# Values of three attention heads projected 512 columns at a time in a one-core hybrid attention and recurrence layer

## The chip, the cores and the metric

The kernel runs on one core of one Trainium2 chip. A core has a matrix engine (TensorE, written PE in the profile, its weight loads PEld), a vector engine (VectorE, DVE), a scalar engine (ScalarE, ACT), GpSimd (POOL) and SyncE (SP), which here only issues DMAs. Each engine works through its own queue in order and waits on semaphores for the others. The metric is the device time of one execution, in microseconds (us).

## The reference, cut to what matters

One layer over 512 latent tokens and 256 context tokens, 2048 features, all in float32. Every token is normalised and modulated, and one input projection makes queries, keys, values, gates and the input of a recurrent branch. What concerns us is the value part `v`, 2048 columns, for four heads of 512 columns each, and for both streams:

```
hn = rmsnorm(h, g_norm) * (1.0 + scale) + shift
parts = split(hn @ w_in, bounds)              # parts[2] is v: GLA_HEADS * GLA_DV = 4 * 512 columns
v = split_heads(parts[2], GLA_DV)
o_gla, ... = gla_bidir(q, k, v, la_f, la_b, s0_f, s0_b)      # attention of each head
y_rnn, ... = rglru_bidir(xc, ...)                             # recurrent branch, 16 blocks of 128 features
out = rmsnorm(x + gt * merge_out(...), g_final)
```

The attention reads `v` of the context and of the latents; the recurrent branch reads neither. So the values can be made anywhere before the head that needs them.

## The kernel before, in words

Every product is made of three matmuls: operands are split into a leading and a remaining part (`hi`, `lo`, type fp32r), and `mm3` (L130) adds hi times hi, hi times lo and lo times hi. ACT makes `whi` from a raw weight piece and DVE makes `wlo` (`hilo`, L121). A piece is [128, 1024] floats, loaded by one DMA; three split pieces are in a ring, and each piece is split two pieces ahead of its matmuls (`run`, L209).

The program has four phases. Phase 0 makes the modulation, the normalised tokens (`xhi`, `xlo` for the latents, `chi`, `clo` for the context) and the keys. Phase 1 makes all that reads the context too: for each of eight `j` a group `g_feat` of the recurrent input (R, both streams), one of its gate (GR, latents only), and after these the groups of values that the table `VALUES_AT` names. Phase 2 makes queries (Q), output gates (G) and merge gates (M) of the latents, 28 groups of 96 matmuls each. Phase 3 is the output projections.

In a group of values before the change (`g_tok`, L273), 256 columns are made at once: the tokens' tile of 128 is the stationary operand, the weights are the moving one, 256 wide. There are eight groups of four pieces; one piece takes 6 token tiles x 4 feature tiles x 3 = 72 matmuls. The sums of four latent tiles lie in two PSUM banks of the pool `px` (four banks), those of the two context tiles in one bank of `pc` (two banks). `evac_v` (L851) then copies bank by bank to `vt` on ACT, two buffers, and POOL sends each `vt` to memory (`vS`), from where the attention reads it back.

Beside the main stream runs side work, written as generators: in phase 1 one `rnn_block` (L898) for each of 16 blocks of the recurrent branch, appended when its GR group ends, and a `gate_row` (L994) at two places; in phase 2 the attention of the four heads (`gla_all`), one after the other. A step of it is put into the program at a `yield` of the main stream, when a rough clock of the engines (`T`, with `rdy`, `lim` and `slack`, in `run_side`, L163) finds that what the step needs will be there. `g_tok` yields after every 6 matmuls of 256 columns. Whatever is left is put in at once, ready or not, by `flush_side` (L199): at the first piece of phase 2 (`to_gla`) and when the first piece of phase 3's input is loaded (`swap`), because the memory pools of the finished phase are closed there. In between, `need` forces side steps where a buffer must be free.

Names in the rows: `rx` and `rc` are the block products of `rnn_block` (latents and context; four pairs in a block, each pair in the same two banks `sa` and `sb`), `g` what ACT makes of them, `xc`, `xh`, `xl`, `wr`, `wh`, `wl` their operands; `pr` and `grow` belong to `gate_row`, whose one `grow` buffer is sent to memory twice, and `pr` uses bank `sa` too; `po` are the output sums of a head, `dg` with `oss` their squares, `on` the normalised sums, `pt` their transposes, `sgg` the gated result.

Of the kernel before, what the change touches and what calls it, by code (L numbers as in the profile page):

```python
# [5 lines left out]
F32 = mybir.dt.float32  # L6
# [6 lines left out]
P = 128  # L13
# [8 lines left out]
# columns of the packed per-feature parameters  # L22
# [5 lines left out]
# weight pieces: [128, 1024] each  # L28
# [13 lines left out]
# the modulation's blocks of feature tiles, and the runs (group, feature tiles) of the keys' products that follow  # L42
# [3 lines left out]
# which groups of the values follow a group of the recurrent branch  # L46
VALUES_AT = [(), (0,), (1,), (2,), (3,), (4,), (), (5, 6, 7)]
# [8 lines left out]
class Kern:  # L56
    def __init__(self, tc, a, out):
        self.tc, self.nc, self.a, self.out = tc, tc.nc, a, out
        self.side = []
        self.pend = ()  # L60
        # a rough clock of the engines as the program is written down: when each is done with what it was given,
        # and when each tile is ready
        self.T = {"pe": 0.0, "dve": 0.0, "act": 0.0}
        self.rdy = {}
        self.table = None
        self.lim, self.slack = 4.0, 1.0
        self.conv_done = self.gr_done = self.q_done = self.heads_done = 0

# [55 lines left out]
    def mm(self, out, lhsT, rhs, start, stop, share=1):  # L124
        # share: how many column tiles of the array work at once
        n = self._n(rhs)
        self._op("pe", (n / 2400.0 + 0.003 if n >= 256 else 0.213) / share, out, lhsT, rhs)
        self.nc.tensor.matmul(out, lhsT=lhsT, rhs=rhs, start=start, stop=stop, skip_group_check=True)  # L128
# [7 lines left out]
    def rstd(self, out, ss, n, tmp):  # L136
        # 1/sqrt(ss/n + eps), the estimate polished by one Newton step
        v, y = tmp[:, 0], tmp[:, 1]
        self.ts(v, ss, 1.0 / n, EPS, ALU.mult, ALU.add)
        self.act(y, v, AF.Sqrt)  # L140
        self.nc.vector.reciprocal(out=y, in_=y)
        self.tt(out, y, y, ALU.mult)
        self.tt(out, out, v, ALU.mult)
        self.ts(out, out, -0.5, 1.5, ALU.mult, ALU.add)
        self.tt(out, out, y, ALU.mult)

# [37 lines left out]
    @staticmethod  # L184
    def zipg(*gens):
        """emit independent chains in turns."""
        gens = list(gens)
        while gens:
            for g in list(gens):
                try:  # L190
                    yield next(g)
                except StopIteration:
                    gens.remove(g)
# [10 lines left out]
    def prime(self, pieces):  # L204
        """the first pieces of the stream to come."""
        self.primed = len(pieces)
        for p in pieces:
            self.load(p)
        return lambda: [self.do_split(p) for p in pieces]  # L209
# [28 lines left out]
    def g_feat(self, w0, evac, ctx, pre=None):  # L238
        """two feature tiles of 128 columns, features on partitions."""
# [33 lines left out]
    def g_tok(self, w0, evac):  # L273
        """256 columns, tokens on partitions, both streams."""
        st = {}
        ps = []

        def mk(pi):
            def mm(hi, lo):
                if pi == 0:  # L280
                    st["x"] = [self.px.tile([P, 2, 256], F32, tag="px", name="px") for _ in range(2)]
                    st["c"] = self.pc.tile([P, 2, 256], F32, tag="pc", name="pc")
                h = hi.rearrange("p (k c) -> p k c", c=256)
                l = lo.rearrange("p (k c) -> p k c", c=256)
                for seg in range(3):
                    for kk in range(4):
                        if kk or seg:
                            yield
                        k = pi * 4 + kk
                        for j in range(2):  # L290
                            if seg < 2:
                                o, t0, xh, xl = st["x"][seg], (2 * seg + j) * P, self.xhi, self.xlo
                            else:
                                o, t0, xh, xl = st["c"], j * P, self.chi, self.clo
                            self.mm3(o[:, j, :], (xh[:, k, t0:t0 + P], xl[:, k, t0:t0 + P]),
                                     (h[:, kk, :], l[:, kk, :]), k == 0 and j == 0, k == KT - 1)
            return mm

        for pi in range(4):
            ps.append(Piece(self.a["w"][w0 + pi], mk(pi), (lambda: evac(st["c"], *st["x"])) if pi == 3 else None))  # L300
        return ps

# [1 line left out]
    def build(self):  # L304
# [44 lines left out]
        # phase 0: modulation, normalised tokens, keys  # L349
# [17 lines left out]
        # phase 1: everything that reads the context as well  # L367
        pcs[0].before = to_rnn
        main = []
        for j in range(8):  # L370
            main += self.g_feat(W_R + 4 * j, self.evac_r(j), True)
            main += self.g_feat(W_GR + 4 * j, self.evac_gr(j), False)
            for i in VALUES_AT[j]:
                main += self.g_tok(W_V + 4 * i, self.evac_v(i))
# [8 lines left out]
        # phase 2: projections of the latents only, attention beside them  # L383
# [22 lines left out]
        # phase 3: output projections  # L406
# [52 lines left out]
    def start(self, sp, raw0, raw, prime):  # L459
        """modulation, normalised tokens in feature-major form, and the keys, whose products follow the tokens  # L460
        feature tile by feature tile: the features come in chunks, and between chunks partial sums wait in SBUF."""
# [18 lines left out]
        # columns c, cctx, and zeros  # L480
# [11 lines left out]
        # the tokens, features on partitions: two feature tiles of the latents or four of the context in each  # L492
# [6 lines left out]
        todo = []          # [earliest start, task] of other engines than the tensor engine  # L499
        hot = []           # the same of the tensor engine, to be done at once  # L500
        rk = {}            # when feature tile (k, stream) is split
# [37 lines left out]
        def rstd(s, r):  # L539
            # the sum of squares of each token on its own partition, and 1/sqrt(mean + eps)  # L540
# [16 lines left out]
        def spread(s, g, r):  # L557
            # the factors of all tokens along the free axis, on every partition
# [50 lines left out]
        def ada():  # L609
# [8 lines left out]
            for kk in range(kn):  # L618
                # four parts of the sum in the array's four column tiles
# [56 lines left out]
        for c, (g, ks) in enumerate(runs):  # L676
            its = [(k, s, c2) for k in ks for s in range(2) for c2 in range(2)]
            if c == 0:
                # the latents of two tiles before the context
                its[2:6] = its[4:6] + its[2:4]  # L680
# [17 lines left out]
        def ksplit_soon():  # L698
            # a piece can be split when its load is there and a place in the ring is free
# [20 lines left out]
        def where(g):  # L720
            """where the sums of a group wait: four banks of the latents, two of the context, in place of what
            has become of the tokens."""
# [96 lines left out]
    def la_pieces(self):  # L819
        st = {}  # L820
        ps = []
        for pi in range(2):
            def conv(raw, pi=pi):
                # columns of each 128: the weights' leading parts three times, their remainders once
# [17 lines left out]
            def post():  # L842
                # rows 0-63 the leading products rounded (twice), 64-95 what the rounding left, 96-127 the others
# [7 lines left out]
    def evac_v(self, j):  # L851
        def f(c, x0, x1):
            h, o = j // 2, (j % 2) * 256
            for i, t in enumerate((c, x0, x1)):
                s = self.rp.tile([P, 2, 256], F32, tag="stg", name="vt", bufs=2)
                self.act(s, t)
                self.nc.gpsimd.dma_start(out=self.vS[h, :, 2 * i:2 * i + 2, o:o + 256], in_=s)
        return f
# [22 lines left out]
    def decay_consts(self):  # L881
        """-8 * softplus(-lam), log1p by the odd series of atanh."""
# [165 lines left out]
    def gla_z(self, h):  # L1048
        """pre-activations of the log decays of head h."""
# [17 lines left out]
    def gla_log(self, h):  # L1067
        """log decays times 16, summed along each block of 128 tokens."""
# [35 lines left out]
    def gla_scores(self, h):  # L1104
# [16 lines left out]
        def make_ctx(d):  # L1121
            """queries and keys whose products reach over to the context, queries' own blocks."""
# [6 lines left out]
            # decays over whole blocks between the pair: context to latents, latents' blocks, context's blocks  # L1129
# [82 lines left out]
        def make_qd(d):  # L1212
            """diagonal blocks, decays against the middle of the block."""
# [44 lines left out]
        def mm_diag(d):  # L1258
# [13 lines left out]
            # key index on partitions, query index on the free axis  # L1272
# [153 lines left out]
    def g_final(self, j):  # L1426
# [13 lines left out]
        def loads(pi):  # L1440
            # a part beside each of the first pieces
# [28 lines left out]
        for pi in range(8):  # L1470
# [26 lines left out]
            def post():  # L1497
# [3 lines left out]
                if j == 2:  # L1501
                    # sums of squares so far, with eps
# [7 lines left out]
    def finish(self, t):  # L1510
# [12 lines left out]
        if t < 3:  # L1523
            # the vector engine has the next tile's sums to take up
# [16 lines left out]
def pack(i):  # L1541
    """Lay the inputs out for the chip: pieces in the order in which they are read."""
# [5 lines left out]
    def g256(w):  # [2048, n*256] -> [n*4, 128, 1024]  # L1548
# [3 lines left out]
    def g512(w):  # [2048, n*512] -> [n*8, 128, 1024]  # L1552
# [3 lines left out]
    c = lambda a, b: w_in[:, a:b]  # L1556
    w = np.concatenate([
        g512(c(1024, 2048)), g256(c(2048, 4096)), g256(c(6176, 8224)), g256(c(8224, 10272)),
# [55 lines left out]
```

## Time and profile before

| what | value |
|---|---|
| median of 3 runs | 2339.16 us (2339.06 to 2339.24) |
| span of the profiled execution | 2337.9 us from first to last instruction |
| PE busy | 2291.6 us, 98% |
| DVE busy | 1153.3 us, 49% |
| ACT busy | 1004.6 us, 43% |

The profile gives the span of one execution. The runs' median lies 1.3 us above it, which is what lies around the first and the last instruction and is taken to stay. A matmul's duration in the trace is longer than the distance to the next one, since matmuls overlap: what a matmul costs is read from the starts of a run of them. An engine's idle time is listed with what ended it.

### The profile page before, as it was taken

The page shows a single profiled execution, that of the slowest core. Times are in us where ns is not written, and L with a number is a line of the kernel's source. Part 1 is how long each engine was busy: PE and PEld are TensorE (multiplying, and loading weights), DVE is VectorE, ACT ScalarE, POOL GpSimd, SP SyncE. Part 2 cuts the span into 40 slices and gives each one's busy share as a digit, 9 for nine tenths or more (in the row PEclk, how much of TensorE's full clock was granted, in tenths as well). Part 3 has the DMA queues.
Part 4 walks back from the last instruction along what each step waited for, and adds up shares of the span by engine and source line. Part 5 has one row for each costly group of instructions (what it writes and reads, how often), then busy time and mean ns, then how long its engine had stood idle before and what let it go on. Part 6 is the DMA issues. An engine that isn't in the chain of part 4 may idle for free. (4 is left out here: it accounts for less than half of the span.)

```text
span 2337.9 us, 29156 instructions
## 1 busy us (share of the span) xinstructions
PE 2291.6 (98%) x12008; PEld 1919.1 (82%) x12008; DVE 1153.3 (49%) x1464; ACT 1004.6 (43%) x1309; POOL 137.3 (6%) x217
## 2 busy tenths in 40 slices
PE   4999999999999999999999999999999999999998
PEld 2557889899988988998888888888888888888786
DVE  5223345566555665555645637637633423434334
ACT  4222244554545545556545646564534311222223
POOL 1222000000000000000000000000000000000000
PEclk8999999999999999999999999999999999999999
DMA  7663323333333333223233233223335533333523
GB/s 299 239 221 118 108 70 107 122 104 119 114 116 104 113 126 109 77 95 128 93 131 108 77 122 117 93 97 118 105 114 200 196 118 118 117 126 136 191 92 117
DMA packets 84406, 296.72 MB, mean 127 GB/s; under 512 B 10160, under 2 KB 11312, under 8 KB 83376
## 3 DMA queue, kind: packets, MB, share of 16 engines
q1 hardware_dynamic: 72656, 256.04, 31.9%
q0 software_dynamic: 11616, 38.81, 4.7%
q8 instruction: 94, 1.54, 0.3%
q14 instruction: 40, 0.33, 0.0%
HBM read 264.40 MB, written 30.42 MB: 126 GB/s over the span
## 5 line engine op out<-in xcount | busy, mean ns | idle before, releaser
L95 DVE TENSOR_TENSOR wlo<-raw,whi 128x1024 fp32r<-128x1024 f32 x304 | 374.8, 1234 | 569.7 <-ACT whi L91 568.2
L91 ACT ACTIVATE whi<-raw 128x1024 fp32r<-128x1024 f32 x304 | 320.8, 1057 | 538.0 <-PE px L128 329.5
L128 PE MATMUL px<-xhi,whi 128*128 128x512 f32 x1408 | 551.5, 392 | 0.0
L128 PE MATMUL px<-xhi,wlo 128*128 128x512 f32 x1408 | 549.0, 390 | 0.0
L128 PE MATMUL px<-xlo,whi 128*128 128x512 f32 x1408 | 548.1, 389 | 0.0
L128 PEld LDWEIGHTS px<-xhi,wlo 128*128 128x128 f32 x1408 | 264.2, 188 | 57.3
L128 PEld LDWEIGHTS px<-xhi,whi 128*128 128x128 f32 x1408 | 264.4, 188 | 54.0 <-issue 2.6
L128 PEld LDWEIGHTS px<-xlo,whi 128*128 128x128 f32 x1408 | 264.4, 188 | 51.6
L128 PE MATMUL px<-whi,xhi 128*128 128x256 f32 x512 | 144.8, 283 | 0.0
L128 PE MATMUL px<-wlo,xhi 128*128 128x256 f32 x512 | 144.8, 283 | 0.0
L128 PE MATMUL px<-whi,xlo 128*128 128x256 f32 x512 | 144.7, 283 | 0.0
L91 ACT ACT_TABLE_LOAD x101 | 129.6, 1283 | 1.8
L128 PE MATMUL px<-wlo,mhi 128*128 128x512 f32 x256 | 101.1, 395 | 0.8 <-DVE wlo L95 0.8
L128 PE MATMUL px<-whi,mhi 128*128 128x512 f32 x256 | 101.1, 395 | 0.0
L128 PE MATMUL px<-whi,mlo 128*128 128x512 f32 x256 | 101.0, 394 | 0.0
L128 PE MATMUL px<-yhi,whi 128*128 128x512 f32 x256 | 100.9, 394 | 0.0
L128 PE MATMUL px<-yhi,wlo 128*128 128x512 f32 x256 | 100.4, 392 | 0.0
L128 PE MATMUL px<-ohi,whi 128*128 128x512 f32 x256 | 99.6, 389 | 0.0
L128 PE MATMUL px<-ohi,wlo 128*128 128x512 f32 x256 | 99.6, 389 | 0.0
L128 PE MATMUL px<-olo,whi 128*128 128x512 f32 x256 | 99.6, 389 | 0.0
L128 PE MATMUL px<-ylo,whi 128*128 128x512 f32 x256 | 99.3, 388 | 0.0
L128 PEld LDWEIGHTS px<-wlo,xhi 128*128 128x128 f32 x512 | 98.1, 192 | 0.2
(320 smaller groups left out, 3959.4 us busy)
## 6 DMA issues: line engine op xcount, KB each, us to landing
raw<-in_w SPq DMA_DIRECT2D x304, 512.0 KB, 3.6
araw<-in_wss SPq DMA_DIRECT2D x64, 512.0 KB, 4.9
raw<-in_wgt SPq DMA_DIRECT2D x32, 512.0 KB, 4.2
gS<-mst POOLq DMA_DIRECT2D x32, 256.0 KB, 2.5
gst<-gS POOLq DMA_DIRECT2D x32, 256.0 KB, 3.0
kraw<-in_w POOLq DMA_DIRECT2D x14, 512.0 KB, 5.5
vS<-vt POOLq DMA_DIRECT2D x24, 256.0 KB, 2.8
st<-vS SPq DMA_DIRECT2D x12, 512.0 KB, 4.7
```

The source lines that it names most:

```text
L91: return self.nc.scalar.activation(out=out, in_=in_, func=func, **kw)
L95: return self.nc.vector.tensor_tensor(out=out, in0=in0, in1=in1, op=op)
L128: self.nc.tensor.matmul(out, lhsT=lhsT, rhs=rhs, start=start, stop=stop, skip_group_check=True)
```

## The change

Heads 0, 1 and 3 are projected by a new group `g_head`: 512 columns at once, eight pieces of two feature tiles each, and a PSUM bank for each of the six token tiles (all four of `px` and both of `pc`). Every tile is copied out as soon as its last matmul is issued. Head 2 stays with `g_tok`, in two groups. The table now puts heads 0 and 1 after j = 1 and 3, the halves of head 2 after j = 5 and 7, and head 3 last. `g_head` yields after every 6 matmuls of 512 columns: five times in a piece, where `g_tok` yields eleven times. The weights are laid out on the host to match.

```
-VALUES_AT = [(), (0,), (1,), (2,), (3,), (4,), (), (5, 6, 7)]
+VALUES_AT = [(), (("w", 0),), (), (("w", 1),), (), (("n", 4),), (), (("n", 5), ("w", 3))]
...
+    def g_head(self, w0, evac):
+        st = {}
+        ps = []
+        def mk(pi):
+            def mm(hi, lo):
+                if pi == 0:
+                    st["o"] = [self.px.tile([P, 512], F32, tag="px", name="px") for _ in range(4)] + \
+                              [self.pc.tile([P, 512], F32, tag="pc", name="pc") for _ in range(2)]
+                for t in range(6):
+                    if t:
+                        yield
+                    xh, xl = (self.xhi, self.xlo) if t < 4 else (self.chi, self.clo)
+                    t0 = (t % 4) * P
+                    for kk in range(2):
+                        k = 2 * pi + kk
+                        self.mm3(st["o"][t], (xh[:, k, t0:t0 + P], xl[:, k, t0:t0 + P]),
+                                 (hi[:, kk * 512:(kk + 1) * 512], lo[:, kk * 512:(kk + 1) * 512]), k == 0, k == KT - 1)
+                    if pi == 7:
+                        evac(t, st["o"][t])
+            return mm
+        for pi in range(8):
+            ps.append(Piece(self.a["w"][w0 + pi], mk(pi)))
+        return ps
...
-            for i in VALUES_AT[j]:
-                main += self.g_tok(W_V + 4 * i, self.evac_v(i))
+            for kind, i in VALUES_AT[j]:
+                if kind == "w":
+                    main += self.g_head(W_V + 8 * i, self.evac_head(i))
+                else:
+                    main += self.g_tok(W_V + 4 * i, self.evac_v(i))
...
+    def evac_head(self, h):
+        def f(t, x):
+            s = self.rp.tile([P, 512], F32, tag="stg", name="vt", bufs=2)
+            self.act(s, x)
+            self.nc.gpsimd.dma_start(out=self.vS[h, :, (t + 2) % 6, :], in_=s)
+        return f
```

Since side work is placed by the rough clock, it moves too. Three places show it.

On PE, at the end of phase 1, before the change, the last product pair of the last recurrent block stands among the matmuls of the last value group:

```order
L128 MATMUL px<-whi,xlo 128x256
L128 MATMUL rx<-xh,wh 128x512
L128 MATMUL rx<-xl,wh 128x512
L128 MATMUL rx<-xh,wl 128x512
L128 MATMUL rc<-xh,wh 128x256
L128 MATMUL rc<-xl,wh 128x256
L128 MATMUL rc<-xh,wl 128x256
L128 MATMUL px<-whi,xhi 128x256
```

With the change, on PE, the first pair of the last block stands behind the last matmul of head 3, and the next pair follows at once:

```order
L129 MATMUL pc<-whi,clo 128x512
L129 MATMUL rx<-xh,wh 128x512
L129 MATMUL rx<-xl,wh 128x512
L129 MATMUL rx<-xh,wl 128x512
L129 MATMUL rc<-xh,wh 128x256
L129 MATMUL rc<-xl,wh 128x256
L129 MATMUL rc<-xh,wl 128x256
L129 MATMUL rx<-xh,wh 128x512
```

All four pairs of that block stand there in a row, ahead of the first query matmul, and the first products of the attention follow 126 matmuls after the queries begin, where it was 72. On ACT, at the same place before the change, the last recurrent block is finished when the copies of the last value group come:

```order
L91 ACTIVATE g_8601<-g_8601 128x768
L91 ACTIVATE g_8690<-g_8690 128x768
L91 ACTIVATE whi<-raw 128x1024
L91 ACTIVATE vt<-pc 128x512
L91 ACTIVATE vt<-px 128x512 x2
L91 ACTIVATE whi<-raw 128x1024 x3
```

With the change, on ACT, at that place (a `g` from `rx` and one from `rc` free the banks for the next pair):

```order
L92 ACTIVATE whi<-raw 128x1024
L92 ACTIVATE vt<-px 128x512 x4
L92 ACTIVATE wh<-wr 128x512
L92 ACTIVATE vt<-pc 128x512 x2
L92 ACTIVATE whi<-raw 128x1024
L92 ACT_TABLE_LOAD
L92 ACTIVATE g_7950<-rx,par 128x512
L92 ACTIVATE g_7950<-rc,par 128x256
L92 ACTIVATE g_7961<-rx,par 128x512
```

The last block's `g` now stand behind all six copies of head 3, behind a split and a table load.

On PE, at the end of phase 2, before the change, the transposes of the last head stand among main matmuls (30 of these lie ahead of the first transposes):

```order
L1371 MATMUL pt<-ident,on 128x128 x4
L128 MATMUL px<-xhi,whi 128x512
L128 MATMUL px<-xlo,whi 128x512
L128 MATMUL px<-xhi,wlo 128x512
L128 MATMUL px<-xhi,whi 128x512
L128 MATMUL px<-xlo,whi 128x512
L128 MATMUL px<-xhi,wlo 128x512
L1371 MATMUL pt<-ident,on 128x128 x4
```

With the change, on PE, all 16 stand directly behind the last output sum of that head:

```order
L129 MATMUL po<-ht,Ah 128x512 x2
L129 MATMUL po<-ht,Al 128x512
L1410 MATMUL pt<-ident,on 128x128 x16
L129 MATMUL px<-xhi,whi 128x512
L129 MATMUL px<-xlo,whi 128x512
```

On PE, at the second gate row, before the change, main matmuls follow its two products:

```order
L1000 MATMUL pr<-gacc,ones 1x512 x2
L128 MATMUL px<-xhi,whi 128x512
L128 MATMUL px<-xlo,whi 128x512
L128 MATMUL px<-xhi,wlo 128x512
L128 MATMUL px<-xhi,whi 128x512
```

With the change, on PE, a block product that uses the bank of `pr` follows them:

```order
L1039 MATMUL pr<-gacc,ones 1x512 x2
L129 MATMUL rx<-xh,wh 128x512
L129 MATMUL rx<-xl,wh 128x512
L129 MATMUL rx<-xh,wl 128x512
L129 MATMUL rc<-xh,wh 128x256
```

At the first gate row the two products stood 6 main matmuls apart, with 6 more ahead of the next `rx`; with the change they stand together, with 6 matmuls of 256 columns ahead of the first `rx` of a block, whose `wh` stands on ACT behind both copies to `grow`.

## Rows read from the trace of the kernel before

**Rows 1.** The page: span, busy time by engine, the costliest group on DVE.
```profile
span 2337.9 us, 29156 instructions
PE 2291.6 (98%) x12008; PEld 1919.1 (82%) x12008; DVE 1153.3 (49%) x1464; ACT 1004.6 (43%) x1309; POOL 137.3 (6%) x217
...
L95 DVE TENSOR_TENSOR wlo<-raw,whi 128x1024 fp32r<-128x1024 f32 x304 | 374.8, 1234 | 569.7 <-ACT whi L91 568.2
```

**Rows 2.** Windows of phase 1 and of the last products: length, busy, clock, DMA.
```profile
561.00:1050.00 489.00, 487.18 (x3193) 443.45 (x3192) 285.45 (x313) 250.34 (x325) 21.19 (x33) 1.00 0.32 107
2060.00:2300.00 240.00, 239.24 (x1036) 193.84 (x1035) 99.54 (x111) 59.39 (x77) 8.38 (x8) 1.00 0.38 131
```

**Rows 3.** Timeline of PE in a value group: start, duration, engine, output and operands.
```profile
395.39 0.28 PE L128 MATMUL px<-whi,xhi 128*128 128x256 f32 x1
...
401.15 0.28 PE L128 MATMUL pc<-whi,chi 128*128 128x256 f32 x1
...
403.98 0.40 PE L128 MATMUL px<-xhi,whi 128*128 128x512 f32 x1
```

**Rows 4.** Timeline of PE, 512 columns: a feature group, then the last products.
```profile
347.05 0.39 PE L128 MATMUL px<-xhi,whi 128*128 128x512 f32 x1
...
349.77 0.39 PE L128 MATMUL px<-xhi,whi 128*128 128x512 f32 x1
...
2260.21 0.39 PE L128 MATMUL px<-whi,mhi 128*128 128x512 f32 x1
...
2279.81 0.39 PE L128 MATMUL px<-whi,mhi 128*128 128x512 f32 x1
```

**Rows 5.** Timelines of ACT and PE: value copies, and a group's last matmul.
```profile
407.73 0.60 ACT L91 ACTIVATE vt<-px 128x512 f32<-128x512 f32 x1 [2.47 <-DMA vS<-vt]
...
1007.44 0.60 ACT L91 ACTIVATE vt<-px 128x512 f32<-128x512 f32 x1 [4.28 <-DMA vS<-vt]
...
963.37 0.28 PE L128 MATMUL pc<-whi,clo 128*128 128x256 f32 x1
...
963.69 0.60 ACT L91 ACTIVATE vt<-pc 128x512 f32<-128x512 f32 x1 [6.23 <-PE pc L128]
...
968.15 0.60 ACT L91 ACTIVATE vt<-px 128x512 f32<-128x512 f32 x1 [3.38 <-DMA vS<-vt]
```

**Rows 6.** Timeline of ACT: a split, a table load, two copies of block products.
```profile
1012.61 1.05 ACT L91 ACTIVATE whi<-raw 128x1024 fp32r<-128x1024 f32 x1
1013.67 1.28 ACT L91 ACT_TABLE_LOAD   x1
...
410.59 0.69 ACT L91 ACTIVATE g<-rx,par 128x512 f32<-128x512 f32 x1
...
412.34 0.69 ACT L91 ACTIVATE g<-rx,par 128x512 f32<-128x512 f32 x1 [0.69 <-PE rx L128]
```

**Rows 7.** Timelines of PE, ACT and DVE behind the last head's sums.
```profile
1721.05 0.39 PE L128 MATMUL px<-xhi,whi 128*128 128x512 f32 x1
...
1721.31 0.60 ACT L91 ACTIVATE dg<-po 128x512 f32<-128x512 f32 x1 [3.39 <-PE po L128]
...
1724.56 1.41 DVE L100 TENSOR_SCALAR on<-po,ors 128x512 f32<-128x512 f32 x2
...
1727.87 1.03 PE L1371 MATMUL pt<-ident,on 128*128 128x128 f32 x8
...
1729.11 0.74 DVE L100 TENSOR_SCALAR on<-po,ors 128x512 f32<-128x512 f32 x1
```

**Rows 8.** Timelines of PE and ACT at the two gate rows.
```profile
651.45 0.50 PE L128 MATMUL rx<-xh,wh 128*128 128x512 f32 x1 [0.85 <-ACT grow L91]
...
915.74 1.02 PE L1000 MATMUL pr<-gacc,ones 128*1 128x512 f32 x2 [0.97 <-ACT grow L91]
...
650.81 0.59 ACT L91 ACTIVATE grow<-pr 1x512 f32<-1x512 f32 x1 [3.73 <-DMA rS<-grow]
...
917.63 0.59 ACT L91 ACTIVATE grow<-pr 1x512 f32<-1x512 f32 x1 [1.94 <-DMA rS<-grow]
```

More of the change, by code (lines that the diff above doesn't have):

```diff
@@ L1556, in pack @@
     c = lambda a, b: w_in[:, a:b]
+    wv = [(g256 if h == 2 else g512)(c(2048 + 512 * h, 2560 + 512 * h)) for h in range(4)]
     w = np.concatenate([
-        g512(c(1024, 2048)), g256(c(2048, 4096)), g256(c(6176, 8224)), g256(c(8224, 10272)),
+        g512(c(1024, 2048)), *wv, g256(c(6176, 8224)), g256(c(8224, 10272)),
         g256(c(0, 1024)), g256(c(4096, 6144)), g256(c(10272, 12320)), g256(c(12320, 14368)),
```

## The prediction

> **What bounds the kernel now.** I read the page first: PE is busy 98% of the span, and no other engine half of it or much over [rows 1]. So I asked for windows. In phase 1 PE is busy 487.2 of 489.0 us at a granted clock of 1.00, that is the 2.4 GHz level, and in the last products 239.2 of 240.0 [rows 2]. PE's time is the time: a stretch gets shorter only if its matmuls do, and every us in which PE waits is paid in full. Two questions follow: what do 512 columns at once save, and does PE wait anew?
>
> **The matmuls.** Three heads had 6 groups of 4 pieces of 72 matmuls, 1728 of 256 columns; two thirds (1152) go to latent tiles, 576 to the context. They become 3 x 8 x 36 = 864 of 512 columns. Cost is read from starts. In a value group, 48 latent matmuls lie between 395.39 and 401.15, 0.1200 us each, and 24 of the context between 401.15 and 403.98, 0.1179 us each [rows 3]. Removed: 1152 x 0.1200 + 576 x 0.1179 = 206.1 us. The trace has no matmul of 512 columns with a tile of xhi as its weights, so I bound it. A feature group runs at (349.77 - 347.05) / 12 = 0.2267 us, the last products, which also rotate token tiles as weights against halves of a ring piece, at (2279.81 - 2260.21) / 84 = 0.2333 us [rows 4]. Added: 195.9 to 201.6 us, a saving of 4.5 to 10.2 us. The last products are the nearer form; I take 0.2315, hence 200.0 us and a saving of 6.1 us.
>
> Both widths thus pay 12 to 20 ns beyond their columns' streaming at 2.4 GHz (0.1067 and 0.2133 us) [rows 3, 4]. The Trainium skill's page "TensorE: Matmul & The Clock Gate", section "Back-to-back issue gap", gives columns / 2.4 + 2.5 ns for a warm isolated gap. By that a pair of narrow ones costs 218.3 ns, a wide one 215.8, and the change would save 2.6 ns x 864 = 2.2 us, an estimate from the page; my sum would end at 2356.5. The rows do not agree with its 2.5 ns, so the sum does not use it.
>
> Splits, piece loads (8 per head before and after) and the copies' total size stay, beside PE's work as before. Five yields in a piece where there were eleven cost nothing by themselves; they change where side work stands.
>
> **Where PE will wait anew.** Four places, each following from an order of instructions.
>
> *End of phase 1.* All four `rx`/`rc` pairs of the last recurrent block now stand behind head 3's last matmul, with nothing of the main stream between them. A pair needs the banks that ACT's two copies of the pair before free, and ACT has head 3's six copies, a split and a table load ahead of these. A copy may start when its buffer, used two copies ago, is sent. From the end of a buffer's copy to its next use it took 2.47 + 0.5 = 2.97 us at the shortest (0.5 being the step of the copy between), 968.15 - 964.29 = 3.86, and 4.28 + 0.5 = 4.78 at the longest [rows 5]. Count from head 3's last matmul. Its tiles end 1.38 us apart (6 x 0.23), the first at -6.9; a copy takes 0.6 and starts some 0.2 later. With 2.97 the copies end at -6.1, -4.7, -2.5, -1.1, 1.1 and 2.5. Then the split (1.05) and the table load (1.28) [rows 6] put the first `g` at 4.85. It frees the bank 0.69 us later, at 5.6, when the second pair starts. From one `g` of `rx` to the next is 412.34 - 410.59 = 1.75 us, with PE and ACT waiting for each other [rows 6]; so the fourth pair starts at 9.1 and ends, after 3 x 0.23 + 3 x 0.12 = 1.05 us, at 10.15. Of this 4 x 1.05 = 4.2 is work that was always there. PE waits 5.9 us; with 3.86 it is 7.7, with 4.78 it is 9.5. Head 3's sends go in longer runs of memory, for which I leave 0.6 below. I take 6.3, near the short end, which a send with nothing else in its way shows. Queries queue behind the pairs on PE, and cannot start earlier.
>
> *End of phase 2.* The attention starts later against the main stream (126 matmuls after the queries begin, where it was 72), never regains it, and the last head is flushed: 16 transposes directly behind its sums. They need squares, a mean, a root with a table load, and the normalised tiles. In the trace 30 matmuls cover that. Without them the rows say: PE free at 1721.05, square at 1721.31, the first two normalised tiles done at 1724.56 + 1.41 = 1725.97; then gating, normalising, gating, normalising on DVE, four steps of about 0.63, to 1728.5, and the last four transposes, 0.4: 1728.9 [rows 7]. That is 7.9 us, less the 16 transposes' own 1.6 (eight from 1727.87 took 0.8): 6.3 us. The sums themselves also come early: their third tile of values is split after a weight piece whose ring place the matmuls just ahead free, so a split of 1.05 [rows 6] and two DVE steps of 1.23 [rows 1] end 3.6 us after those, and the sums ask for it after 13 matmuls, 3.0 us: 0.6 more. I take 7.0, range 6.3 to 8.
>
> *Gate rows.* The second copy to `grow` waits until the first is sent, 3.73 us at one row and 1.94 at the other [rows 8]. From the first product's start: product 1.02, copy 0.59, send 1.94 to 3.73, copy 0.59, so the bank is free at 4.2 to 6.0. The two products with their wait end at 2.65. At the second row `rx` follows at once and wants that bank: 1.6 to 3.4 us of new waiting. At the first, 6 narrow matmuls (0.7) follow, and then an `rx` whose `wh` and `wl` (0.6 each, half of a 1024-wide step) come after the second copy: 2.1 to 3.9, and the second product's wait of 0.7 to 0.97, which is new there too, less the 0.85 that this place has now [rows 8]: 2.0 to 4.0. Together 3.6 to 7.4; I take 5.0.
>
> *Into head 3.* It wants all four banks of `px` at once, two of them from the half of head 2 just ahead. That one's last copy ended at 968.75, 5.26 us after its last matmul's slot ended (963.49) [rows 5]; head 3's fourth tile comes after 18 matmuls, 4.16 us. A wait of 1.2 us, 0.2 to 2.1 with the other sends. Heads 0 and 1 take banks from a gate group, whose two copies of 0.6 wait for no DMA and are wanted after 2.8 and 4.2 us: no wait.
>
> **Sum.** -6.1 + 6.3 + 7.0 + 5.0 + 1.2 = +13.4 us on a span of 2337.9; with the 1.3 us around it, which take the span to the runs' median, 2352.6 us. All terms at their good ends: -10.2 + 5.3 + 6.3 + 3.6 + 0.2 = +5.2, 2344.4; at their bad ends: -4.5 + 9.5 + 8 + 7.4 + 2.1 = +22.5, 2361.7.
>
> **Rivals.**
> 1. *The waits are covered.* DVE and ACT are idle half the time [rows 1], so the forced side work might be done when PE comes to it, and only the shorter matmuls count: 2339.2 - 6.1 = 2333.1. It decides if all new waits stay under 1.4 us. If they come to 1.4 to 10.8 (say, both the gate rows and the end of phase 2 covered: -6.1 + 6.3 + 1.2, 2340.6), the time stays as it is. Against both: each wait is a chain through one bank or buffer, and an idle engine doesn't shorten it.
> 2. *Sending takes long.* Copies back to back at 4.78 us, as at 1007.44 [rows 5], and the last but one head forced too (its last transposes come exactly where the next head's gate needs them done): 9.5 + 8 + 7.4 + 2.1 - 6.1 and up to 2 more, some 2362.
> 3. *The clock.* Six banks in turn might make the granted clock fall to the 1.2 GHz level in the heads. In the last products four banks in turn kept it at 1.00 for 240 us [rows 2], which speaks against it. If one tenth of the added 200 us ran at half clock, 20 us come on top: 2373. That cycling through PSUM banks can make the clock go back and forth is what the Trainium skill's page "TensorE: Matmul & The Clock Gate" says in "A second HAM failure mode: psum-queue depth-cycling"; the trace here shows no such case.
>
> **Chances.** Forecast 0.79; rival 2 0.07, rival 3 0.01; unchanged 0.08; faster 0.05. A measurement of this kernel tells about 0.2%, 4.7 us, from no change; the forecast and rivals 2 and 3 lie beyond that, so slower has 0.87. Range 2345 to 2361.
>
> **What would show it.** Right: PE's starts in the heads 0.227 to 0.234 us apart; behind head 3 some 10 us in which PE does four pairs; behind the last `po` some 8 us with 16 transposes; both gate rows with an `rx` waiting for `grow`; a wait at head 3's fourth tile. Wrong: any of the first two stretches without a wait, or wide matmuls outside these bounds; then the term falls with it. Waits for weight splits in the heads would be something I have not priced.

## The result, and the profile after

The changed kernel takes 2371.78 us (median of 4 runs, 2370.48 to 2373.75) against 2339.11 (2338.01 to 2339.24) for the kernel before on the same chip: ratio 1.0138, 95% interval 1.0126 to 1.0151. It is slower, as forecast, but by 32.7 us where 13.4 were forecast, outside the range.

The page of the changed kernel, the answer to [rows 1]:

```profile
span 2368.8 us, 27446 instructions
## 1 busy us (share of the span) xinstructions
PE 2298.2 (97%) x11144; PEld 1883.2 (80%) x11144; DVE 1150.4 (49%) x1464; ACT 1004.7 (42%) x1309; POOL 133.3 (6%) x217
```

PE has 864 matmuls fewer and is busy 6.6 us longer. So PE was in part slower while it was busy, and its waits alone cannot be all. These are the new ones in the list of what PE waited for (us in total, times, longest):

```profile
PE rx L129 <- ACT g L92: 6.3, 3, 3.5
PE rx L129 <- ACT wh L92: 6.1, 2, 3.2
PE pt L1410 <- DVE on L101: 4.8, 2, 4.2
PE px L129 <- ACT vt L92: 3.9, 2, 2.5
...
PE rx L129 <- ACT grow L92: 1.5, 1, 1.5
PE pr L1039 <- ACT grow L92: 1.4, 2, 0.7
```

PE's timeline shows both, the waits and the slowness: a wait behind the first gate row, the matmuls of head 3 at the forecast pace, then the end of phase 1 (start, duration, engine, line, output and operands, idle time before and its releaser):

```profile
657.05 0.80 PE L129 MATMUL rx<-xh,wh 128*128 128x512 f32 x1 [3.22 <-ACT wh L92]
...
1038.77 0.39 PE L129 MATMUL px<-whi,xlo 128*128 128x512 f32 x1
...
1041.49 0.39 PE L129 MATMUL px<-whi,xlo 128*128 128x512 f32 x1
1041.72 0.40 PE L129 MATMUL pc<-whi,chi 128*128 128x512 f32 x1
...
1044.29 0.39 PE L129 MATMUL pc<-whi,clo 128*128 128x512 f32 x1
1047.60 0.50 PE L129 MATMUL rx<-xh,wh 128*128 128x512 f32 x1 [2.92 <-ACT wh L92]
...
1053.31 0.80 PE L129 MATMUL rx<-xh,wh 128*128 128x512 f32 x1 [3.55 <-ACT g L92]
1053.90 0.63 PE L129 MATMUL rx<-xl,wh 128*128 128x512 f32 x1
1054.32 0.63 PE L129 MATMUL rx<-xh,wl 128*128 128x512 f32 x1
...
1060.25 0.63 PE L129 MATMUL px<-xhi,whi 128*128 128x512 f32 x1
```

A wide matmul takes 0.227 us with a latent tile ((1041.49 - 1038.77) / 12) and 0.234 with a context tile ((1044.29 - 1041.72) / 11). But behind the wait for `g`, starts of the same width stand 0.42 to 0.59 us apart. The windows (length, busy time of five engines, granted clock, DMA) say why:

```profile
653.50:657.00 3.50, 0.33 (x3) 0.12 (x2) 0.00 (x0) 1.11 (x2) 0.24 (x1) 0.82 0.31 126
657.00:662.50 5.50, 5.45 (x22) 5.12 (x23) 0.69 (x1) 2.40 (x3) 0.26 (x1) 0.50 0.00 0
662.50:668.00 5.50, 5.50 (x29) 4.61 (x28) 2.18 (x2) 2.12 (x3) 0.00 (x0) 1.00 0.27 84
1038.00:1044.50 6.50, 6.50 (x30) 5.13 (x28) 2.40 (x3) 3.37 (x5) 1.10 (x3) 1.00 0.40 102
...
1053.30:1061.60 8.30, 8.02 (x22) 6.29 (x23) 1.56 (x2) 4.28 (x9) 0.00 (x0) 0.50 0.26 65
...
1764.00:1772.00 8.00, 7.17 (x26) 5.38 (x27) 4.52 (x7) 0.00 (x0) 1.06 (x2) 0.57 0.17 68
1772.00:1778.00 6.00, 6.00 (x28) 4.95 (x27) 1.50 (x2) 2.01 (x2) 0.00 (x0) 1.00 0.21 85
```

In head 3, with six banks in turn, the clock is 1.00, the 2.4 GHz level (it is the same in the other two wide heads). In three places where PE had just waited it is 0.50 to 0.57, all or mostly the 1.2 GHz level, and behind them it is back at 1.00. PE counts as busy there, and so its busy time grew although it had less to do.

Below, excess is the time from each matmul's start to the next, less 0.2275 us for 512 columns, 0.1185 for 256, 0.1 for a transpose and 0.475 for a gate product, summed where it is over 0.06, from 440 us on. It holds waits and slow matmuls alike: 8.6 us before, 47.1 after. Over all starts in the value groups (gaps over 0.3 taken as waits) the wide matmuls take 198.8 us, the narrow ones they replace 205.7: 6.9 saved. 47.1 - 8.6 - 6.9 = +31.6; the spans differ by 30.9. By place (all from the two profiled executions):

| place | forecast | measured, us |
|---|---|---|
| matmuls | -6.1 | -6.9 |
| end of phase 1 | +6.3 | +12.4 |
| end of phase 2, with a wait at 1745 in the sums | +7.0 | 8.7 + 0.6 = +9.3 |
| gate rows | +5.0 | 7.5 + 2.6 - 1.5 - 1.3 = +7.3 |
| into head 3 | +1.2 | +4.4 |
| at 455, 640, 809 and 1643 us, less one wait gone at 2203 | none | 1.7 + 0.8 + 1.8 + 1.6 - 1.3 = +4.6 |
| sum | +13.4 | +31.1 |

### The profile page after: what moved, and what is told of

Its sections match the earlier page's. It is cut to its first block, busy times and chain, and to the rows that moved or that the text cites. A ratio compares the mean times of both kernels' runs of the same rounds, so it can differ in the third digit from the quotient of the medians.

```text
span 2368.8 us, 27446 instructions
## 1 busy us (share of the span) xinstructions
PE 2298.2 (97%) x11144; PEld 1883.2 (80%) x11144; DVE 1150.4 (49%) x1464; ACT 1004.7 (42%) x1309; POOL 133.3 (6%) x217
## 4 chain that ended last, share of the span: by engine, by line
PE 70%; issue 25%; DVE 2%; ACT 1%; POOL 1%; DMA 1%; DVEq 0%; SPq 0%; POOLq 0%; ACTq 0%
PE px L129 53%; PE kx L806 4%; PE po L129 3%; PE kc L806 2%; PE pa L653 2%; PE pc L129 2%; PE pd L129 1%; PE pcs L129 1%; PE rx L129 1%; DVE rms L565 1%; POOL yS L1014 0%; POOL vS L896 0%; PE pt L1410 0%; DMA araw<-in_wss 0%; DMA oS<-sgg 0%
## 5 line engine op out<-in xcount | busy, mean ns | idle before, releaser
L129 PE MATMUL px<-whi,xhi 128*128 128x512 f32 (+1 forms) x320 | 111.6, 349 | 3.9 <-ACT vt L92 3.9
L129 PE MATMUL px<-whi,xlo 128*128 128x512 f32 (+1 forms) x320 | 111.2, 347 | 0.0
L129 PE MATMUL px<-wlo,xhi 128*128 128x512 f32 (+1 forms) x320 | 111.0, 347 | 0.0
L96 DVE TENSOR_TENSOR g<-g,xc 128x768 f32<-128x768 f32 x32 | 30.6, 958 | 141.7 <-ACT g L92 141.7
```

The costliest lines, as they stand in the source:

```text
L96: return self.nc.vector.tensor_tensor(out=out, in0=in0, in1=in1, op=op)
```

## The experiments

An offer is a `yield` of the main stream, at which a step of side work may be put in. A pair is an `rx` with its `rc`; it is forced when it is put in ready or not. Two theories. T1: the width saves what was forecast and costs nothing by itself; what costs is where the values stand and how seldom a wide head offers a place to side work, so that side work comes late and is forced, with waits, and with a slow clock behind long ones. T2: wide heads, with six banks at once and six copies at their end, make PE wait. Ratios are to the kernel before, run on the same chip as each experiment, with 95% intervals. In the tables of places, `n0` stands for `("n", 0)` and `w0` for `("w", 0)`; where a head becomes narrow or wide, its weights are laid out to match.

**E1. Narrow groups in the new places.**
```
VALUES_AT = [(), (n0, n1), (), (n2, n3), (), (n4,), (), (n5, n6, n7)]   # all g_tok, 256 columns
```


> All eight value groups narrow (256 columns, as before), but standing where the change puts its values: halves 0 and 1 behind the second recurrent group, 2 and 3 behind the fourth, 4 behind the sixth, 5, 6 and 7 behind the last. Theory (the places make PE wait, not the width): both gate rows stand directly ahead of an rx again (about 7 us more than before), the last head is flushed at the end of phase 2 (some 8 us), one forced pair at the end of phase 1 (2 to 5 us), no saving of matmuls: 2352 to 2362 us. Rival (wide matmuls with six banks at once make the waits): within 3 us of the kernel before, 2336 to 2342.

2359.57 us, 1.0082 (1.0069 to 1.0094): as T1 said. Excess at the end of phase 2 is 8.4, at the gate rows 3.7 and 2.6, at the end of phase 1 7.0 with one forced pair (2 to 5 were expected there). No matmul is wide in the values.

**E2. More offers.** `g_head` yields after every product (11 in a piece).
```
-                    if t:
-                        yield
...
                     for kk in range(2):
+                        if t or kk:
+                            yield
```


> The changed kernel with a step of side work offered after every product of a wide head's piece (11 in a piece, as two narrow pieces had, instead of 5), all else the same. Theory (fewer offers make the side work late): three of the four forced pairs at the end of phase 1 move up, its 12.4 us become 4 to 6; the first gate row's 7.5 become 1.5 to 3; second gate row, head 3's start and end of phase 2 stay. 2371.8 - 7 - 5 = 2360 us (2356 to 2364). Rival (the number of offers doesn't matter; the width's banks and the copies make the waits): 2369 to 2373.

2352.98 us, 1.0052 (1.0039 to 1.0066): T1's direction, and 3 us below its range. End of phase 1 is 4.0, as expected, the first gate row 0.9, less than expected; the waits at 455 and 640 us went too (2.5). A narrow piece of about the same length in time has eleven offers too, so E1 and E2 differ in the width of three heads alone: the wide twin is 6.6 us faster, with nearly the same excess (28.9 and 29.9). That speaks against T2.

**E3. Matmuls that nobody reads, against the slow clock.**
```
+            if b == 15: self.fill((9, 13, 2, 2)[m])    # ahead of each rx, into a free px bank
...
+        if h == 3: self.fill(14)                       # behind the last po
```


> The changed kernel with matmuls of 512 columns that nobody reads, 9, 13, 2 and 2 of them ahead of the four rx of block 15 at the end of phase 1, and 14 behind the last po of head 3, where PE waits in any case; nothing else moves. Theory (long waits of PE let the granted clock fall to 0.5, and what follows runs at half speed): the clock stays above 0.9 there, the pairs come every 1.75 us instead of 2.43, the end of phase 1 loses 3.5 to 5.5 us, the end of phase 2 1.5 to 3: 2364 us (2362 to 2367). Rival (the clock in those stretches is no matter, since ACT and DVE set their pace): 2370 to 2374, and slower still if the added matmuls stand in the way.

2370.71 us (2366.29 to 2374.03), 1.0127 (1.0113 to 1.0141): by its median the time is the rival's, and the runs reach from T1's range to the rival's. The profiled run is the fastest of them. At the end of phase 2 the clock stayed at 1.00 and excess plus the added matmuls came to 3.4 + 3.2 = 6.6 instead of 8.7, as T1 said. At the end of phase 1 the sixth copy waited 3.68 us for a send, where it had been 1.68; the added matmuls were done 3.3 us too early, and the clock fell all the same. It fell at the start of head 3 too: behind a wait of 2.47 us it is 0.50 from 973 to 979.7, and the excess there is 6.9 instead of 4.4.

**E4. More buffers.** The order on all engines stays.
```
-            s = self.rp.tile([P, 512], F32, tag="stg", name="vt", bufs=2)       # both copy functions
+            s = self.rp.tile([P, 512], F32, tag="stg", name="vt", bufs=4)
...
-            row = self.rp.tile([1, 512], F32, tag="grow", name="grow")
+            row = self.rp.tile([1, 512], F32, tag="grow", name="grow", bufs=2)
```


> The changed kernel with four buffers for the copies of values instead of two, and two for the gate rows' copy instead of one; the order of instructions on every engine is the same. Theory (the copies wait for sends, and PE waits for them): into head 3 4.5 -> 0 to 1, the wait at 640 us gone (0.8), both gate rows without the wait for a send (10 -> 3 to 5, the first without the clock's fall), at the end of phase 1 the copies' 6.4 us of waiting go, worth 3 to 5: 2371.8 - 15 = 2357 us (2353 to 2362). Rival (the sends are not on the path; the banks and the late side work are): 2368 to 2373.

2355.83 us, 1.0065 (1.0053 to 1.0078): as expected, some 16 us of the loss were waits for sends and what follows them. First gate row 7.5 -> 1.8 without a slow clock, second 2.6 -> 1.8, end of phase 1 12.4 -> 6.8, 455, 640 and 809 gone. Into head 3 only 4.4 -> 2.7, where 0 to 1 was expected: the other part is not the sends (below).

**E5. Moved heads, more offers.** E2's yields, and
```
VALUES_AT = [(), (), (n4,), (w0,), (), (w1,), (), (w3, n5)]
```


> Three wide heads and two narrow halves as in the change, but in other places (the narrow half 4 behind the third recurrent group, heads 0 and 1 behind the fourth and sixth, head 3 and then half 5 behind the last) and with an offer of side work after every product of a head's piece (11 in a piece). The gate rows then stand 14 to 29 us of matmuls ahead of the next rx, no pair is forced at the end of phase 1, and 65 products lie between the last sums and the end of their transposes, as in the kernel before. Theory (the width saves some 8 us, and all the rest was late side work): 2339.1 - 8 + 0 to 3 for heads that want four banks at once = 2331 to 2335 us. Rival (six banks at once and 512-wide copies cost about what the width saves): 2338 to 2342.

2333.14 us, 0.9972 (0.9962 to 0.9983): as T1 said. All forecast waits are gone, and the width is left. Beyond the start of the program and small waits that were there before, PE waits for this:

```profile
PE pc L129 <- ACT vt L92: 1.4, 1, 1.4
PE pr L1039 <- ACT grow L92: 0.8, 1, 0.8
PE px L129 <- ACT gr L92: 0.8, 1, 0.8
```

**E6. The same places, narrow.** As E5, all groups `g_tok`.

> The same places as in the kernel with the heads moved (half 4 behind the third recurrent group, 0 and 1 behind the fourth, 2 and 3 behind the sixth, 6, 7 and 5 behind the last), all groups narrow. Theory (places alone are worth nothing here, and the width is worth 8 us): 2337 to 2342 us, and 6 to 9 us above its wide twin. Rival (the places give the gain, not the width): 2331 to 2335, as its twin.

2345.84 us, 1.0028 (1.0017 to 1.0040): above what T1 said, and 12.7 over its wide twin. Excess is 13.8 against 8.6, since the offers fall elsewhere: 2.8 ahead of the first `pz`, 2.4 between two gate products. 6.9 + 5.2 = 12.1 explains the twins' distance; that the places alone are worth nothing was too simple.

**E7. Moved heads, five offers.** E5 without E2's yields.

> The moved heads with only the changed kernel's five offers of side work in a piece. The written order again has all four pairs forced behind the values at the end of phase 1 and the 16 transposes directly behind the last sums; the gate rows stay free. Theory (few offers make the side work late, whatever the places): 2333 + 10 to 12 at the end of phase 1 + 8 to 9 at the end of phase 2 = 2349 to 2357 us. Rival (the places alone decide): 2331 to 2336.

2349.91 us, 1.0046 (1.0034 to 1.0059): T1's, at the low end. The flush at the end of phase 2 is back (8.3), and 3.9 came at 1622. At the end of phase 1 it is 6.5, not 10 to 12: in the trace only the last pair follows its forerunner directly, not all four.

**E8. E5 with E4's buffers.**

> The moved heads with 11 offers, and four buffers for the copies of values and two for the gate rows' copy. Theory (what is left of new waiting is for sends: the second gate product, copies ahead of the last recurrent blocks): 1 to 3 us under the kernel with the heads moved, 2329 to 2334 us. Rival (no wait for a send is left on the path): within 1 us of it.

2331.97 us, 0.9969 (0.9957 to 0.9982): 1.2 under E5, at the low end of what was expected and at the edge of what two medians tell.

**E9. E4 with added matmuls**, 17, 2 and 2 ahead of the second to fourth `rx`, 17 behind the last `po`.

> The changed kernel with the added buffers (four for the values' copies, two for the gate rows'), and matmuls of 512 columns that nobody reads where PE waits in any case: 17, 2 and 2 ahead of the second, third and fourth rx of block 15 (a wait of 4.4 us there without them) and 17 behind the last po of head 3. Theory (a long wait of PE lets the granted clock fall, and the matmuls behind it run at half speed): the clock stays above 0.9 in both places, the half-speed excess there (2.4 and 3.1 us in the kernel with buffers alone) goes, the pairs come every 1.75 us: 2355.8 - 4 to 5 = 2351 to 2352 us. Rival (ACT and DVE set the pace there, the clock adds nothing): 2355 to 2357.

2351.15 us, 1.0047 (1.0035 to 1.0060): the time is T1's. Windows behind the last head's sums (length, busy time, clock, DMA), in E9 and then in E4:

```profile
1746.00:1754.00 8.00, 6.33 (x34) 4.87 (x34) 4.87 (x8) 0.00 (x0) 1.06 (x2) 1.00 0.18 69
```
```profile
1749.00:1757.00 8.00, 7.31 (x25) 5.56 (x26) 4.75 (x8) 0.00 (x0) 1.07 (x2) 0.57 0.15 60
```

Excess plus added matmuls is there 2.7 + 3.9 = 6.6 against 8.5. At the end of phase 1 the clock is 1.00 too (0.70 in E4), and the pairs come every 1.74 us on ACT:

```profile
1039.71 0.69 ACT L92 ACTIVATE g<-rx,par 128x512 f32<-128x512 f32 x1
...
1041.45 0.69 ACT L92 ACTIVATE g<-rx,par 128x512 f32<-128x512 f32 x1 [0.69 <-PE rx L129]
...
1044.93 0.69 ACT L92 ACTIVATE g<-rx,par 128x512 f32<-128x512 f32 x1 [0.69 <-PE rx L129]
```

But from the last value matmul to the first query it is 10.5 us against 11.2. So the two places gave 1.9 + 0.7. Later waits went as well (1.5 at a `pz`, 1.7 for splits at 1628, less 1.0 at 2216), which makes 4.8 in all; E9's profiled execution was 0.9 slower at the start of the program (last key matmul at 240.9 us, not 240.0), and 3.8 are left between the two spans. Why the later waits went stays open: of E9's gain over E4, only 2.6 is shown to be the clock's.

**E10. Four wide heads**, E2's yields, E4's buffers.
```
VALUES_AT = [(), (), (w0,), (w1,), (), (), (), (w2, w3)]
```


> All four heads wide (heads 0 and 1 behind the third and fourth recurrent groups, 2 and 3 behind the last), 11 offers of side work in a piece, the added buffers. Theory: a third of the 6.9 us that three wide heads save, 2.3 us, comes on top of 2332.0 for the moved heads with buffers, less 1 to 3 for head 3, which takes its four banks directly behind head 2's, and for recurrent pairs that stand closer: 2330 to 2333 us. Rival (the fourth head's direct succession makes PE wait for six copies): 2335 or more.

2345.11 us, 1.0025 (1.0016 to 1.0034): T1's forecast missed by 12 us; the rival has the time, but not the place that it named. PE stands 8.4 us in a recurrent group, because `need` (a buffer of `xr`) forces side work ahead of the copies and the split; its lines on PE and ACT:

```profile
876.61 0.80 PE L129 MATMUL px<-xhi,whi 128*128 128x512 f32 x1 [8.44 <-ACT whi L92]
```
```profile
874.01 0.84 ACT L92 ACTIVATE xh<-xc 128x768 fp32r<-128x768 f32 x1 [8.73 <-DVE xc L106]
```

Behind it the clock is 0.50 for 5.4 us (876.6 to 882).

**E11. Head 1 one group later.** As the program is written down, `need` forces no step in the kernel before, in E5, E6 and E8; four steps at two places of phase 2 in the changed kernel, E1, E2, E4 and E7; 13 in E10. Of all places for four wide heads in order with the last behind the last group, this one alone forces none:
```
VALUES_AT = [(), (), (w0,), (), (w1,), (), (), (w2, w3)]
```


> As the kernel with four wide heads, but head 1 stands behind the fifth recurrent group instead of the fourth. Written so, no step of side work is forced into the main stream (13 are there with head 1 behind the fourth, 4 in the changed kernel, none in the kernel before and in the moved heads with 11 offers). Theory (what costs is side work that has to be forced; wide matmuls only save): the waits of 8.6, 2.9 and 3.5 us around 868 to 897 us go; the first gate row stands directly ahead of an rx, 1 to 2 us with two buffers; 2332.0 - 2.2 + 1 to 2 = 2329 to 2332 us. Rival (heads 2 and 3 in direct succession, or the fourth wide head as such, cost what the width saves or more): 2335 to 2345.

2330.08 us, 0.9961 (0.9948 to 0.9975): as T1 said, and the fastest of the kernels here.

The same sum for all but E3 and E9 (it does not hold their added matmuls): 2337.9 + excess - 8.6, less the saving of the wide matmuls (6.9 for three heads, none in E1 and E6, 9.1 for four, whose value matmuls take 265.1 us instead of 274.2):

| | E1 | E2 | E4 | E5 | E6 | E7 | E8 | E10 | E11 |
|---|---|---|---|---|---|---|---|---|---|
| excess | 28.9 | 29.9 | 30.4 | 8.6 | 13.8 | 27.7 | 7.5 | 24.1 | 7.5 |
| span by it | 2358.2 | 2352.3 | 2352.8 | 2331.0 | 2343.1 | 2350.1 | 2329.9 | 2344.3 | 2327.7 |
| span | 2358.7 | 2353.2 | 2353.8 | 2332.3 | 2342.5 | 2349.9 | 2330.3 | 2344.6 | 2327.0 |

All lie within 1.3 us: the saving goes with the number of wide heads wherever they stand, and the excess decides.

## Why the prediction was right in sign and wrong in size

**Matmuls: right.** 6.9 against 6.1, between the bounds. By the isolated gap that the Trainium skill's page "TensorE: Matmul & The Clock Gate", section "Back-to-back issue gap", gives, it would have been 2.2, an estimate; the runs bear out the rows instead. The third rival (six banks in turn let the clock fall) is out: 1.00 in the heads. Two slips in the working change no sum: what both widths pay over streaming is 11 to 20 ns by the rows, not 12, and 218.3 less 215.8 is 2.5, not 2.6.

**The step that failed: a wait was priced at its own length.** All four places were named and all four have their wait. What stood nowhere in the sum is the slow clock behind a long one. "From one `g` of `rx` to the next is 412.34 - 410.59 = 1.75 us" was taken from a stretch at full clock; at half clock it was this, on ACT:

```profile
1039.07 1.04 ACT L92 ACTIVATE whi<-raw 128x1024 fp32r<-128x1024 f32 x1
1040.03 1.06 ACT L92 ACTIVATE vt<-px 128x512 f32<-128x512 f32 x2
1043.58 0.60 ACT L92 ACTIVATE vt<-px 128x512 f32<-128x512 f32 x1 [2.49 <-DMA vS<-vt]
1046.43 0.60 ACT L92 ACTIVATE vt<-px 128x512 f32<-128x512 f32 x1 [2.26 <-DMA vS<-vt]
1046.93 0.62 ACT L92 ACTIVATE wh<-wr 128x512 fp32r<-128x512 f32 x1
...
1049.71 0.60 ACT L92 ACTIVATE vt<-pc 128x512 f32<-128x512 f32 x1 [1.68 <-DMA vS<-vt]
...
1052.57 0.69 ACT L92 ACTIVATE g<-rx,par 128x512 f32<-128x512 f32 x1
...
1054.99 0.69 ACT L92 ACTIVATE g<-rx,par 128x512 f32<-128x512 f32 x1 [1.37 <-PE rx L129]
...
1059.85 0.69 ACT L92 ACTIVATE g<-rx,par 128x512 f32<-128x512 f32 x1 [1.31 <-PE rx L129]
```

Three periods take 7.28 us where E9's take 5.22: 2.1, and the first four queries 0.8 more: 2.8 together. At the end of phase 2 it is 1.9 to 2.1 (E3, E9), at the first gate row 2.7 (the slow matmuls from 657 to 662.5, gone in E4). That is some 7.5 of the 17.7 us that the sum lacked. E3 and E9 show the part at the end of phase 2 and the pace of the pairs; the rest is read from rows. At the end of phase 1, E9 against E4 gives 0.7 for the clock where it was slow in fewer matmuls, so 2.8 is not shown by itself. The Trainium skill's page "TensorE: Matmul & The Clock Gate", section "HAM oscillation — how this bites in real kernels", says of a loop that waits for DMAs that the wait takes TensorE back to the slow clock and the next work starts slow. Here 5.5 us of matmuls at 0.50 behind a wait of 3.2, for ACT, agree with it. The prediction had weighed what that page of the Trainium skill says of banks and passed over this.

**End of phase 1, the copies' chain: 3.3 more.** The first `g` came 8.05 us after the end of head 3's last matmul (1052.57 - 1044.52), not 4.85. The first copy started 2.2 late, behind a split on ACT at 1039.07. From a buffer's copy to its next use it took 3.0, 5.3, 3.3 and 2.7 us; I had taken 2.97 for each, and 5.3 is beyond the long end (4.78) too, so a range from three rows of the kernel before was too narrow; the second rival (long sends) had this part, and 2362 in all. For the 0.6 that was left for head 3's longer runs of memory no run has a sign: these four sends show nothing shorter than 2.7. `wh`, which the first `rx` needs, stands behind the fourth copy. That wait (2.92) was missing, but it set no time: the first `g` came 5 us after that `rx` started, held by the copies, the split and the table load.

**Into head 3: 3.2 more.** The half of head 2 ends 4.3 us before its first copy starts (973.88 - 969.62), since ACT has late side work ahead of it; I had taken the copies where the rows of before have them. So PE waits at the third tile already, which was to be free, and again at the fourth. PE, then ACT:

```profile
975.00 0.50 PE L129 MATMUL px<-whi,xhi 128*128 128x512 f32 x1 [2.47 <-ACT vt L92]
...
978.08 0.50 PE L129 MATMUL px<-whi,xhi 128*128 128x512 f32 x1 [1.42 <-ACT vt L92]
```
```profile
973.88 0.58 ACT L92 ACTIVATE vt<-pc 128x512 f32<-128x512 f32 x1
974.36 0.59 ACT L92 ACTIVATE vt<-px 128x512 f32<-128x512 f32 x1
977.43 0.60 ACT L92 ACTIVATE vt<-px 128x512 f32<-128x512 f32 x1 [2.48 <-DMA vS<-vt]
```

The last line's wait is for a send; without it (E4) 1.7 us go and 2.7 stay.

**Waits that were not priced: 4.6.** I looked where the order puts a need directly behind its cause. These four are side work or copies that stand a little later everywhere.

**Gate rows and end of phase 2: right but for the clock.** 7.3 - 2.7 = 4.6 against 5.0, and 9.3 - 2.0 = 7.3 against 7.0. PE at the end of phase 2, the answer to [rows 7], has 8.4 us between the last sum's end (1759.43 + 0.23) and the next main matmul, 7.9 forecast, with the transposes behind two waits for `on`:

```profile
1759.43 0.39 PE L129 MATMUL po<-ht,Al 128*128 128x512 f32 x1
1763.97 1.42 PE L1410 MATMUL pt<-ident,on 128*128 128x128 f32 x8 [4.15 <-DVE on L101]
1766.07 2.37 PE L1410 MATMUL pt<-ident,on 128*128 128x128 f32 x8 [0.68 <-DVE on L101]
1768.09 0.78 PE L129 MATMUL px<-xhi,whi 128*128 128x512 f32 x1
```

Adding up clock, copies' chain, head 3, waits not priced, gate rows, end of phase 2 and matmuls: 7.5 + 3.3 + 3.2 + 4.6 - 0.4 + 0.3 - 0.8 = 17.7, which is 31.1 less 13.4. The clock is thus the largest single part and less than half. The statement "Five yields in a piece where there were eleven cost nothing by themselves" held as to their own cost, and it hid the main thing: E2 against the changed kernel and E7 against E5 price their effect on the order at 19 and 17 us.

## What to carry to other kernels

Where one engine is busy 98% of the time and side work is threaded into it, a change of a main loop's step is first a change of the places that side work gets: count them, and the steps that must be forced, before and after, and put them back (E5, E11) before judging the change. Price a wait of PE of several us with the matmuls behind it at half speed, and take every duration used there from rows at the clock that will hold there. Waits of some 2.5 us went either way here, so such a term needs a range with both. A chain through two buffers wants the longest turnaround in the trace as its far end, and more.

## Not expected of the hardware

- After PE's waits of 3.2 to 8.4 us the granted clock was 0.50 to 0.57 in the windows behind them, and matmuls of 512 columns started 0.43 us apart instead of 0.23; added matmuls in such a wait kept it at 1.00 (E3 at the end of phase 2, E9).
- Shorter waits of one length did not all do the same. Into head 3 PE waits 2.47 us in the changed kernel and E4, and the clock stays at 1.00 behind it; in E2 it is 0.50 from 968 to 971.2, in E3 from 973 to 979.7, behind a wait as long at the same place. A wait of 2.63 us in E6 left it at 1.00.
- PE's busy time grew by 6.6 us with 864 matmuls fewer, so busy time alone does not tell work from slowness.
- A matmul of 512 columns took 0.227 us with latent tiles as weights (the median; 0.2285 in the mean) and 0.233 with context tiles, two of 256 columns 0.240 and 0.235: nearly all the gain of the width is with the latent tiles.
